# A one-core decoder layer: norm factors in PSUM, x in halves, four projection tiles moved, sums of weights one at a time

## The chip, the cores and the metric

The kernel runs on one core of a Trainium2 chip, all arithmetic in fp32. The metric is the device time of one launch in microseconds. TensorE is PE here, VectorE DVE, ScalarE ACT, GpSimd POOL, and SP is the engine that issues the DMAs.

## What is computed

One step of a decoder layer for a prompt of 1024 tokens and 8 samples of 4 tokens, 1056 columns in all, model width 1024:

```
hn  = rms_norm(x, norm_mix_pre)
mix = hybrid_mixer(hn, states)            # three head groups, one output projection w_out
x   = x + rms_norm(mix, norm_mix_post)
hn  = rms_norm(x, norm_ffn_pre)
gate, val = split(hn @ w_up)              # 1024 -> 2 x 2816
gate = causal_dwconv(gate)                # width 3
f   = (gelu(gate) * val) @ w_down         # 2816 -> 1024
y   = x + rms_norm(f, norm_ffn_post)
```

and the updated states of prompt and samples.

## The kernel before

Activations lie transposed: 128 of the 1024 features on the partitions, tokens along the free axis. The 1056 columns are cut into four quarters of 264 (Q). A weight tile is 128 outputs wide; it is loaded in fp32, cast by ACT to a rounded high part wh, and the remainder wl is a subtraction on POOL or DVE (`load_w`, L263 to L273). A product (`dense`, L275) takes three matmuls for each of 8 k-steps: high by high, high by low, low by high, 24 matmuls for one tile and one quarter.

PE's order is the order in which the program emits its instructions. The other engines are ordered by a scheduler from emission order and priorities; `tc.high_priority(offset=n)` moves instructions n places ahead. The emission is done by `Weave` (L121): each stream is a generator with a rank, it yields the nanoseconds or the condition that it waits for, and a virtual clock (`weave.now`) is advanced by the matmuls emitted. The stream of lowest rank that is due goes next, so streams of high rank fill the gaps. The due times are the table WAIT.

The stages that matter:

- **Samples.** The samples' states are worked through in `sample_gdn`, `sample_ssd` and `sample_ml` (ranks 3 to 5), while `project_first` (L1638, rank 9) fills the gaps with w_out's products for quarters 0 and 1. Behind the first tile it splits quarter 2's input (`split_mix(2)`: two casts, two subtractions).
- **Projection.** `project_last` (L1656) does all eight tiles for quarters 2 and 3. Its weights, and the first four gate tiles of w_up (`load_up`), are loaded between the products. `product` (L1592) has ACT read a result from PSUM twice (L1596, L1599), and POOL sums the squares of two tiles at a time (L1601). PSUM has two banks in `accp`, one in `sump`, and in this stage five in `accr`.
- **Norms.** `finish(q)` (L1603, rank 8) waits for the quarter before, loads x of the quarter into the one tile x, and makes the factor r of the first norm with `rstd_of` (L310): two matmuls with ones, logarithm and exponential on ACT, r in SBUF. Then mix is scaled (L1616), x added (L1617), squared and summed (L1620, L1624), x1 written to DRAM, and after `f_rows[q]` nanoseconds the second norm follows: its sum on PE, r, a product (L1634) and a split in two parts (L1580, L1581).
- **Up projection.** Four gate tiles are done as plain products, quarter by quarter (`up`, L1930), into the four fpre tiles of `new_pre` (L1802; POOL sets their first columns at L1779). `pieces` (L1703) makes seven combinations of the input's halves, and the other tiles are done in pairs by a scheme of seven products (class `fast`, L1867): a task is a pair of gate or of value tiles, its steps (p, u) are product p for half u of the columns, 12 matmuls each. Products 4 and 3 of a task are done within the steps of the next task. `weights(p)` makes the weight combinations on DVE (L1883, L1884, L1886, L1888), priority AHEAD = 400, then casts and subtracts (L1849, L1850). Results leave PSUM through DVE (L1824, L1826, L1833 for value tiles).
- **Down projection.** w_down is done in six parts; L2016 adds a product onto fa. In the last part `final(q)` (L2026) scales fa by the norm's weights on ACT (L2030), makes r, and multiplies and adds x on DVE and POOL (L2034, L2035).

Of the kernel before, what the change touches and what calls it, by code (L numbers as in the profile page):

```python
# [73 lines left out]
    s_norm=6310, rows1=9000, rows2=6960, rows3=8500, f_rows=(24000, 15500, 15500, 12500), f_wait=7000, f_piece=2600,  # L74
# [123 lines left out]
def kernel(ctx: ExitStack, tc: tile.TileContext, I, O):  # L198
# [111 lines left out]
    def rstd_of(r, ssum):  # L310

        ps = sump.tile([P, 512], F32, name="po")
        n = r.shape[-1]
        for s in ssum:
            mm(ps[:, :n], lhsT=ones, rhs=s, start=(s is ssum[0]), stop=(s is ssum[-1]))
        log = nc.scalar.activation(out=r, in_=ps[:, :n], func=AF.Ln, scale=1.0 / D, bias=epsc)
        in_order(log, tables[-1])
        nc.scalar.activation(out=r, in_=r, func=AF.Exp, scale=-0.5)
        return r
# [51 lines left out]
    with ExitStack() as ph:  # L371
# [1220 lines left out]
        def product(m, w, q):  # L1592
            if m == 0:
                sqs[q] = on.tile([P, 2, Q], F32, name="ss", bufs=4)
            ps = yield from dense(accp if q < 2 else accr, w, operand, KS, q, Q)
# [7 lines left out]
        def finish(q):  # L1603
            if q:
                yield lambda: ("x", q - 1) in have
            x = on.tile([P, KD, Q], F32, name="x")
            dma(out=x, in_=I["xQ"][q])
            yield WAIT["f_wait"]
            s = sqs[q]
            r = rstd_of(on.tile([P, Q], F32, name="rstd", bufs=2), [s[:, 0, :], s[:, 1, :]])  # L1610
            sx = on.tile([P, KH, Q], F32, name="sx")
            s = on.tile([P, 2, Q], F32, name="ss", bufs=4)
            for i in range(2):
# [3 lines left out]
                vtt(out=x[:, ks], in0=x[:, ks], in1=m, op=ALU.add)  # L1617
                if i == 0:
                    act(out=sx, in_=x[:, ks], func=AF.Square)
                    vtt(out=sx[:, 0:2], in0=sx[:, 0:2], in1=sx[:, 2:4], op=ALU.add)  # L1620
                else:
                    for a in (KH, KH + 2):
                        act(out=sx[:, 2:4], in_=x[:, a:a + 2], func=AF.Square)
                        vtt(out=sx[:, 0:2] if a == KH else s, in0=sx[:, 0:2], in1=sx[:, 2:4], op=ALU.add)  # L1624
                dma(out=x1_dram[q, :, ks], in_=x[:, ks])
            for k in range(KD):
                act(out=mix[k][:, quarters[q]], in_=x[:, k, :], func=AF.Copy, scale=col(V_FPRE + k))
            have.add(("x", q))
            yield WAIT["f_rows"][q]
            r = rstd_of(on.tile([P, Q], F32, name="rstd", bufs=2), [s[:, 0, :], s[:, 1, :]])  # L1630
# [7 lines left out]
        def project_first():  # L1638
            for m in range(KD):
                w = load_w(I["w_out"][m], KD)  # L1640
                for q in range(2):
                    yield from product(m, w, q)
                if m == 0:
                    split_mix(2)
# [529 lines left out]
```

## Time and profile before

| | us |
|---|---|
| median of 3 runs | 1590.47 |
| lowest, highest | 1586.07, 1594.12 |
| the profiled execution | 1597.13 |
| its span | 1595.3 |
| PE busy | 1480.2 (93%) |
| DVE busy | 1014.4 (64%) |
| ACT busy | 621.1 (39%) |
| POOL busy | 581.2 (36%) |

Times in the rows are microseconds from the span's start. A row of the timeline has the start, the duration, the engine, the line, the operation with its output and inputs, the count where rows are merged, and in brackets the idle time before it with the instruction that ended it. Matmul ends are modelled, so that consecutive matmuls overlap in their rows.

### The profile page before, as it was taken

What the parts mean: (1) busy time and instruction counts of PE and PEld (TensorE: products, weight loads), DVE (VectorE), ACT (ScalarE), POOL (GpSimd) and SP (SyncE); (2) the same over time, 40 slices, a digit from 0 to 9 for tenths busy, and PEclk for the clock granted to TensorE, in tenths of its full rate; (3) what the DMA queues carried; (4) which work ended last, traced back from release to release, by engine and by line L of the source; (5) the groups of instructions that cost most, each with busy time, mean ns of one, the idle gap of its engine ahead of it and who ended that gap; (6) DMA issues with size and microseconds to landing.
All of it is one profiled execution on the core that took longest, in us unless ns stands there. A gap on an engine that the chain in (4) does not pass through costs nothing. (4 is left out here: it accounts for less than half of the span.)

```text
span 1595.3 us, 27520 instructions
## 1 busy us (share of the span) xinstructions
PE 1480.2 (93%) x10756; PEld 1430.2 (90%) x10756; DVE 1014.4 (64%) x2019; ACT 621.1 (39%) x1348; POOL 581.2 (36%) x666
## 2 busy tenths in 40 slices
PE   9888998989989989998599999999999999999995
PEld 8888898979989889887499999999999999999995
DVE  6898878795484367513688766666666675234457
ACT  7643544433432332413556533333333344112244
POOL 6344333232444542437240533333332332212323
PEclk9899999999999999769799999999999999999998
DMA  6110111011121232213531212221222226312303
GB/s 217 33 45 29 32 37 37 22 30 30 56 61 40 69 112 83 68 53 98 196 110 57 77 59 67 81 81 68 81 74 75 81 92 233 122 50 94 119 28 137
DMA packets 59786, 124.92 MB, mean 78 GB/s; under 512 B 15480, under 2 KB 21496, under 8 KB 58632
## 3 DMA queue, kind: packets, MB, share of 16 engines
q1 hardware_dynamic: 59656, 123.16, 23.2%
q8 instruction: 85, 1.39, 0.4%
q14 instruction: 45, 0.37, 0.1%
HBM read 97.40 MB, written 25.21 MB: 77 GB/s over the span
## 5 line engine op out<-in xcount | busy, mean ns | idle before, releaser
L208 PE MATMUL acc<-h,wh 128*128 128x264 f32 (+1 forms) x3040 | 687.1, 317 | 15.8 <-DVE pre L308 11.7
L208 PEld LDWEIGHTS acc<-h,wh 128*128 128x128 f32 x3040 | 505.4, 195 | 23.3 <-DVE pre L308 8.0
L208 PE MATMUL acc<-h,wl 128*128 128x264 f32 (+1 forms) x1528 | 471.4, 308 | 2.9 <-POOL wl L272 2.4
L208 PEld LDWEIGHTS acc<-h,wl 128*128 128x128 f32 x1528 | 295.5, 193 | 3.9 <-POOL wl L272 2.6
L208 PE MATMUL acc<-hidl,wh 128*128 128x264 f32 x576 | 163.7, 284 | 0.5 <-DVE hidl L1993 0.5
L208 PE MATMUL acc<-hidh,wh 128*128 128x264 f32 x576 | 163.9, 285 | 0.0
L208 PE MATMUL acc<-hidh,wl 128*128 128x264 f32 x576 | 163.5, 284 | 0.0
L1850 POOL TENSOR_TENSOR wl<-ws,wh 128x512 fp32r<-128x512 f32 x60 | 77.6, 1301 | 191.2 <-ACT wh L1849 191.2
L2016 DVE TENSOR_TENSOR fa<-fa,acc 128x264 f32<-128x264 f32 x160 | 68.0, 427 | 124.5 <-PE acc L208 123.7
L272 POOL TENSOR_TENSOR wl<-w,wh 128x1024 fp32r<-128x1024 f32 x42 | 104.7, 2493 | 54.3 <-ACT wh L271 50.8
L208 PE MATMUL acc<-n,wh 128*128 128x264 f32 x640 | 119.3, 283 | 0.0
L208 PEld LDWEIGHTS acc<-hidl,wh 128*128 128x128 f32 x576 | 108.5, 188 | 0.8 <-DVE hidl L1993 0.8
L208 PEld LDWEIGHTS acc<-hidh,wl 128*128 128x128 f32 x576 | 108.6, 189 | 0.0
L208 PEld LDWEIGHTS acc<-hidh,wh 128*128 128x128 f32 x576 | 108.5, 188 | 0.0
L208 PE MATMUL acc<-r,wh 128*128 128x264 f32 x480 | 91.0, 287 | 13.3 <-DVE rs L1826 13.3
L2007 POOL TENSOR_TENSOR wl<-w,wh 128x1024 fp32r<-128x1024 f32 (+1 forms) x22 | 47.6, 2163 | 148.3 <-ACT wh L2006 145.4
L208 PEld LDWEIGHTS acc<-n,wh 128*128 128x128 f32 x640 | 98.8, 188 | 0.2 <-issue 0.2
L208 PE MATMUL acc<-n,wl 128*128 128x264 f32 x320 | 92.0, 288 | 3.1 <-POOL wl L1850 3.1
L1850 POOL TENSOR_TENSOR wl<-w,wh 128x512 fp32r<-128x512 f32 x40 | 59.2, 1488 | 81.8 <-ACT wh L1849 81.8
L208 PEld LDWEIGHTS acc<-r,wh 128*128 128x128 f32 x480 | 74.3, 188 | 15.4 <-DVE rs L1826 15.2
L1786 DVE SCALAR_TENSOR_TENSOR fy<-fpre,vec,fy 128x1072 f32<-128x1072 f32 x44 | 67.3, 1548 | 14.9 <-ACT fy L217 14.8
L2006 ACT CAST wh<-w 128x1024 fp32r<-128x1024 f32 (+1 forms) x22 | 20.5, 933 | 131.7 <-PE acc L208 127.0
(527 smaller groups left out, 3073.2 us busy)
## 6 DMA issues: line engine op xcount, KB each, us to landing
w<-in_w_in_dram SPq DMA_DIRECT2D x30, 512.0 KB
w<-in_w_up_dram SPq DMA_DIRECT2D x60, 256.0 KB
hid_dram<-hid SPq DMA_DIRECT2D x22, 528.0 KB
hidl<-hid_dram SPq DMA_DIRECT2D x21, 528.0 KB
w<-in_w_dn_dram SPq DMA_DIRECT2D x17, 512.0 KB
w<-in_w_out_dram SPq DMA_DIRECT2D x16, 512.0 KB
E<-rows_dram SPq DMA_DIRECT2D x24, 256.0 KB
n<-in_w_up_dram SPq DMA_DIRECT2D x20, 256.0 KB
```

Source lines behind the costliest of these rows:

```text
L208: return nc.tensor.matmul(out, **kw)
L272: tt(out=wl[:, ks], in0=w[:, ks], in1=wh[:, ks].bitcast(F32), op=ALU.subtract)
L1786: stt(out=y[:, :LF], in0=pre[:, j:j + LF], scalar=col(V_FW + 3 * f + j), in1=y[:, :LF], op0=ALU.mult, op1=ALU.add)
L1850: tt(out=wl, in0=x, in1=wh.bitcast(F32), op=ALU.subtract)
L2006: nc.scalar.copy(out=wh, in_=w)
L2007: gtt(out=wl, in0=w, in1=wh.bitcast(F32), op=ALU.subtract)
L2016: vtt(out=fa[:, q, m, :], in0=fa[:, q, m, :], in1=ps[:, :Q], op=ALU.add)
```

## The change

- `rstd_of` can leave r in the PSUM bank of its sum. All factors of `finish` and `final` do so, the first of `finish` in `sump`, the others in `accp`.
- x of a quarter is loaded in two halves, x0 and x1. Quarter 1 has homes of its own in two fpre tiles, from when the left pool is closed. The due times f_rows change.
- `project_first` also does tiles 0 to 3 for quarter 2; weights 2 and 3 are held in the homes h4 to h7 of quarter 1's operands. `split_mix(2)` is behind the fourth tile, and the second tile's load is raised by 300 places. `project_last` loads tiles 4 to 7 at its start and does those for quarter 2, then all eight for quarter 3. Tiles 4 and 7 take their subtraction on DVE.
- The four sums of weights of a task are methods of their own, called one by one between steps at normal priority; the next task's tiles are allocated and loaded from the fifth step of the one before, and its outputs' tiles at first use.
- `final` multiplies by the norm's weights and r in one DVE instruction; the adds are on POOL, except six of the last quarter's on DVE.

```diff
@@ -71,7 +71,7 @@
     ssd_unit=6650, ssd_post=2800, s_decay=3970, state=430, s_hop=2530, outer=760, s_ml=3230, s_out=2100,
-    s_norm=6310, rows1=9000, rows2=6960, rows3=8500, f_rows=(24000, 15500, 15500, 12500), f_wait=7000, f_piece=2600,
+    s_norm=6310, rows1=9000, rows2=6960, rows3=8500, f_rows=(20000, 22000, 16000, 12500), f_wait=7000, f_piece=2600,
 )
@@ -307,13 +307,15 @@
-    def rstd_of(r, ssum):
-        ps = sump.tile([P, 512], F32, name="po")
-        n = r.shape[-1]
+    def rstd_of(r, ssum, pool=sump, name="po"):
+        n = ssum[0].shape[-1]
+        ps = pool.tile([P, 512], F32, name=name)[:, :n]
         for s in ssum:
-            mm(ps[:, :n], lhsT=ones, rhs=s, start=(s is ssum[0]), stop=(s is ssum[-1]))
-        log = nc.scalar.activation(out=r, in_=ps[:, :n], func=AF.Ln, scale=1.0 / D, bias=epsc)
+            mm(ps, lhsT=ones, rhs=s, start=(s is ssum[0]), stop=(s is ssum[-1]))
+        r = ps if r is None else r
+        log = nc.scalar.activation(out=r, in_=ps, func=AF.Ln, scale=1.0 / D, bias=epsc)
         in_order(log, tables[-1])
@@ -1589,10 +1591,10 @@
-        def product(m, w, q):
+        def product(m, w, q, pool):
             if m == 0:
                 sqs[q] = on.tile([P, 2, Q], F32, name="ss", bufs=4)
-            ps = yield from dense(accp if q < 2 else accr, w, operand, KS, q, Q)
+            ps = yield from dense(pool, w, operand, KS, q, Q)
             act(out=mix[m][:, quarters[q]], in_=ps[:, :Q], func=AF.Copy, scale=col(V_NPOST + m))
@@ -1601,33 +1603,37 @@
         def finish(q):
-            if q:
-                yield lambda: ("x", q - 1) in have
-            x = on.tile([P, KD, Q], F32, name="x")
-            dma(out=x, in_=I["xQ"][q])
+            yield lambda: "left" in have if q == 1 else q == 0 or ("x", q - 1) in have
+            xs = [new_pre()[:, :KH * Q].rearrange("p (k g) -> p k g", k=KH) if q == 1 else
+                  on.tile([P, KH, Q], F32, name=f"x{i}") for i in range(2)]
+            for i in range(2):
+                dma(out=xs[i], in_=I["xQ"][q][:, KH * i:KH * i + KH])
+            if q == 1:
+                yield lambda: ("x", 0) in have
             yield WAIT["f_wait"]
             s = sqs[q]
-            r = rstd_of(on.tile([P, Q], F32, name="rstd", bufs=2), [s[:, 0, :], s[:, 1, :]])
+            r = rstd_of(None, [s[:, 0, :], s[:, 1, :]])
             sx = on.tile([P, KH, Q], F32, name="sx")
...
                 vtt(out=m, in0=m, in1=bc(r, 1, KH), op=ALU.mult)
-                vtt(out=x[:, ks], in0=x[:, ks], in1=m, op=ALU.add)
+                vtt(out=xs[i], in0=xs[i], in1=m, op=ALU.add)
+                dma(out=x1_dram[q, :, ks], in_=xs[i])
                 if i == 0:
-                    act(out=sx, in_=x[:, ks], func=AF.Square)
+                    act(out=sx, in_=xs[i], func=AF.Square)
                     vtt(out=sx[:, 0:2], in0=sx[:, 0:2], in1=sx[:, 2:4], op=ALU.add)
                 else:
-                    for a in (KH, KH + 2):
-                        act(out=sx[:, 2:4], in_=x[:, a:a + 2], func=AF.Square)
-                        vtt(out=sx[:, 0:2] if a == KH else s, in0=sx[:, 0:2], in1=sx[:, 2:4], op=ALU.add)
-                dma(out=x1_dram[q, :, ks], in_=x[:, ks])
+                    for a in (0, 2):
+                        act(out=sx[:, 2:4], in_=xs[i][:, a:a + 2], func=AF.Square)
+                        vtt(out=s if a else sx[:, 0:2], in0=sx[:, 0:2], in1=sx[:, 2:4], op=ALU.add)
             for k in range(KD):
-                act(out=mix[k][:, quarters[q]], in_=x[:, k, :], func=AF.Copy, scale=col(V_FPRE + k))
+                act(out=mix[k][:, quarters[q]], in_=xs[k // KH][:, k % KH], func=AF.Copy, scale=col(V_FPRE + k))
             have.add(("x", q))
             yield WAIT["f_rows"][q]
-            r = rstd_of(on.tile([P, Q], F32, name="rstd", bufs=2), [s[:, 0, :], s[:, 1, :]])
+            r = rstd_of(None, [s[:, 0, :], s[:, 1, :]], accp, "acc")
             new_operand(q)
@@ -1635,43 +1641,52 @@
+        def tile_w(t):
+            return t[:, :D].rearrange("p (k c) -> p k c", c=P)
+        held = {}
+        def hold(m, parts=None):
+            held[m] = load_w(I["w_out"][m], KD, parts=parts, tt=vtt if m in (4, 7) else gtt)
...
             for m in range(KD):
-                w = load_w(I["w_out"][m], KD)
+                with tc.high_priority(offset=300) if m == 1 else nullcontext():
+                    w = load_w(I["w_out"][m], KD)
                 for q in range(2):
-                    yield from product(m, w, q)
-                if m == 0:
+                    yield from product(m, w, q, accp)
+                if m == 3:
                     split_mix(2)
...
             for m in range(2):
-                held[m] = load_w(I["w_out"][m], KD)
+                hold(m)
+            for m in range(2, 4):
+                hold(m, [tile_w(hnp.tile([P, T], F32R, name=f"h{2 * m + i}")) for i in range(2)])
+            for m in range(4):
+                yield from product(m, held[m], 2, accp)
             have.add("half")
...
-        def tile_w(t):
-            return t[:, :D].rearrange("p (k c) -> p k c", c=P)
-        held = {}
...
             def load(m):
-                parts = [tile_w(new_n((2 * m + 4) % 12 + i)) for i in range(2)]
-                held[m] = load_w(I["w_out"][m], KD, parts=parts, tt=vtt if m % 2 else gtt)
+                hold(m, [tile_w(new_n(2 * m - 8 + i)) for i in range(2)])
...
                 held["up", f] = load_w(I["w_up"][2 * f], KD, parts=parts)
-            load(2)
+            for m in range(4, KD):
+                load(m)
             split_mix(3)
-            for q in (2, 3):
-                for m in range(KD):
-                    yield from product(m, held[m], q)
-                    if q == 2 and m + 3 < KD:
-                        load(m + 3)
-                    if q == 3 and m < PLAIN:
-                        load_up(m)
-                weave.add(finish(q), 8)
+            for m in range(4, KD):
+                yield from product(m, held[m], 2, accr)
+            weave.add(finish(2), 8)
+            for m in range(KD):
+                yield from product(m, held[m], 3, accr)
+                if m < PLAIN:
+                    load_up(m)
+            weave.add(finish(3), 8)
             have.add("projected")
@@ -1697,6 +1712,8 @@
+        have.add("left")
@@ -1709,6 +1726,8 @@
                 X[u][p] = hi, lo
+            for q in range(2 * u, 2 * u + 2):
+                yield lambda: ("normed", q) in have
             vtt(out=B[0][0], in0=B[0][1], in1=B[0][0], op=ALU.subtract)
@@ -1732,7 +1751,8 @@
             yield from pieces(0, {p: [(fn, f"n{2 * i + j}") for j in range(2)] for i, p in enumerate((6, 5, 7, 4))})
-            yield lambda: ("normed", 3) in have
+            for q in range(NQ):
+                yield lambda: ("normed", q) in have
             onstack.close()
@@ -1803,9 +1823,11 @@
         def gate_task(i):
-            pres = [new_pre() for j in range(2)]
+            pres = []
...
             def out(j, h, u, x, ps):
+                if not pres:
+                    pres.extend(new_pre() for j in range(2))
                 gate_in(pres[j], 2 * u + h, x, ps)
@@ -1814,9 +1836,11 @@
         def value_task(i):
-            hids = [fo[0].tile([P, T], F32, name="hid", bufs=2) for j in range(2)]
+            hids = []
...
             def out(j, h, u, x, ps):
+                if not hids:
+                    hids.extend(fo[0].tile([P, T], F32, name="hid", bufs=2) for j in range(2))
                 q = 2 * u + h
@@ -1872,20 +1896,26 @@
                 self.A = [[w[j][:, KH * r:KH * r + KH] for j in range(2)] for r in range(2)]
-                for r, j in ((0, 0), (1, 0), (1, 1), (0, 1)):
+                for r, j in ((1, 0), (1, 1), (0, 0), (0, 1)):
                     dma(out=self.A[r][j], in_=I["w_up"][2 * (2 * i + r) + val][:, KH * j:KH * j + KH])
...
+            def sum_of(self, n):
+                A = self.A
+                if n == 0:
+                    self.s = [fo[0].tile([P, KH, P], F32, name="ws", bufs=3)]
+                    vtt(out=self.s[0], in0=A[1][0], in1=A[1][1], op=ALU.add)
+                elif n == 1:
+                    self.s.append(fo[0].tile([P, KH, P], F32, name="ws", bufs=3))
+                    vtt(out=self.s[1], in0=self.s[0], in1=A[0][0], op=ALU.subtract)
+                elif n == 2:
+                    vtt(out=A[1][0], in0=A[0][0], in1=A[1][0], op=ALU.subtract)
+                else:
+                    vtt(out=self.s[1], in0=A[0][1], in1=self.s[1], op=ALU.subtract)
...
                 A = self.A
-                if p == 6:
-                    self.s = [fo[0].tile([P, KH, P], F32, name="ws", bufs=3) for j in range(2)]
-                    vtt(out=self.s[0], in0=A[1][0], in1=A[1][1], op=ALU.add)
-                    vtt(out=self.s[1], in0=self.s[0], in1=A[0][0], op=ALU.subtract)
-                elif p == 7:
-                    vtt(out=A[1][0], in0=A[0][0], in1=A[1][0], op=ALU.subtract)
-                elif p == 3:
-                    vtt(out=self.s[1], in0=A[0][1], in1=self.s[1], op=ALU.subtract)
                 x = {1: A[0][0], 2: A[0][1], 4: A[1][1], 7: A[1][0]}.get(p)
@@ -1946,15 +1976,18 @@
             prev = None
+            following = tasks[0][0](tasks[0][1])
+            for k in range(2):
+                following.sum_of(k)
             for n, (task, i) in enumerate(tasks):
-                cur = task(i)
+                cur = following
                 if n == 0:
...
                             drain(gate_conv(2 * i + j, pres[2 * i + j], ys[i][j]))
-                for p, u in ((1, 0), (1, 1), (6, 0), (4, 0), (4, 1), (3, 0), (6, 1), (3, 1),
-                             (5, 0), (5, 1), (2, 0), (2, 1), (7, 0), (7, 1)):
+                for at, (p, u) in enumerate(((1, 0), (1, 1), (6, 0), (4, 0), (4, 1), (3, 0), (6, 1), (3, 1),
+                                             (5, 0), (5, 1), (2, 0), (2, 1), (7, 0), (7, 1))):
                     if p in (4, 3):
@@ -1964,6 +1997,13 @@
                         one_later()
+                    if at in (0, 8):
+                        cur.sum_of(3 if at else 2)
+                    elif n + 1 < len(tasks):
+                        if at == 4:
+                            following = tasks[n + 1][0](tasks[n + 1][1])
+                        elif at in (9, 10):
+                            following.sum_of(at - 9)
                 prev = cur
@@ -2026,13 +2066,12 @@
             dma(out=x, in_=x1_dram[q])
+            r = rstd_of(None, ssum[q], accp, "acc")
             for k in range(KD):
-                act(out=fa[:, q, k, :], in_=fa[:, q, k, :], func=AF.Copy, scale=col(V_FPOST + k))
-            r = rstd_of(fp.tile([P, Q], F32, name="rstd", bufs=2), ssum[q])
-            for k in (0, 2, 1, 3, 4, 6, 5, 7):
-                tt = gtt if k in ((2, 5) if q == NQ - 1 else (1, 2, 5)) else vtt
-                tt(out=fa[:, q, k, :], in0=fa[:, q, k, :], in1=r, op=ALU.mult)
-                tt(out=x[:, k, :], in0=x[:, k, :], in1=fa[:, q, k, :], op=ALU.add)
+                y = fa[:, q, k, :]
+                stt(out=y, in0=y, scalar=col(V_FPOST + k), in1=r, op0=ALU.mult, op1=ALU.mult)
+                tt = vtt if q == NQ - 1 and k not in (1, 4) else gtt
+                tt(out=x[:, k, :], in0=x[:, k, :], in1=y, op=ALU.add)
                 yield
...
```

## Rows read from the trace of the kernel before

**Rows 1.** The page, its slices of the span

```profile
PEclk9899999999999999769799999999999999999998
```

**Rows 2.** What PE waited for: us, times, longest

```profile
PE po L208 <- DVE ss L1624: 15.4, 1, 15.4
PE acc L208 <- DVE rs L1826: 13.3, 9, 1.7
...
PE acc L208 <- POOL wl L1850: 3.6, 11, 0.6
```

**Rows 3.** Windows by stage: length, busy PE PEld DVE ACT POOL, clock, DMA

```profile
640.00:658.00 18.00, 14.52 (x105) 13.65 (x103) 16.54 (x34) 14.02 (x30) 6.95 (x6) 1.00 0.26 85
658.00:704.00 46.00, 46.00 (x211) 41.58 (x212) 4.96 (x16) 6.72 (x17) 17.93 (x19) 0.50 0.13 45
704.00:749.00 45.00, 43.74 (x324) 39.51 (x323) 14.25 (x26) 13.69 (x36) 30.05 (x20) 0.98 0.25 83
749.00:762.00 13.00, 9.17 (x23) 3.84 (x23) 7.22 (x10) 4.75 (x7) 6.55 (x4) 0.87 0.48 162
762.00:782.00 20.00, 18.57 (x148) 18.02 (x146) 18.50 (x13) 13.04 (x22) 8.59 (x4) 1.00 0.59 194
782.00:804.00 22.00, 6.24 (x18) 4.87 (x19) 8.67 (x9) 11.63 (x27) 2.59 (x2) 0.55 0.53 190
804.00:888.00 84.00, 81.55 (x654) 80.64 (x654) 69.77 (x53) 52.13 (x96) 28.75 (x26) 1.00 0.21 73
```

**Rows 4.** Windows, two tasks of the up projection

```profile
993.40:1036.62 43.22, 41.26 (x338) 40.84 (x337) 28.06 (x50) 14.62 (x24) 14.79 (x19) 1.00 0.22 75
```

**Rows 5.** Timeline, the wait in that period

```profile
992.24 1.76 DVE L1883 TENSOR_TENSOR ws<-w 128x512 f32<-128x512 f32 x1 [1.43 <-POOL wl L1850]
...
995.47 0.42 DVE L1826 TENSOR_TENSOR rs<-n,acc 128x264 f32<-128x264 f32 x1
...
995.94 0.51 PE L208 MATMUL acc<-r,wh 128*128 128x264 f32 x2 [1.65 <-DVE rs L1826]
```

**Rows 6.** Timeline, w_out's second tile

```profile
653.47 3.21 POOL L272 TENSOR_TENSOR wl<-w,wh 128x1024 fp32r<-128x1024 f32 x1 [0.71 <-POOL kqM L1389]
...
656.73 0.39 PE L208 MATMUL acc<-h,wl 128*128 128x264 f32 x1 [2.37 <-POOL wl L272]
```

**Rows 7.** Timeline of PE, state matmuls of the samples

```profile
662.02 0.85 PE L208 MATMUL mc<-kqS,kq 128*128 128x8 f32 x4
...
664.20 0.85 PE L208 MATMUL mc<-kqS,kq 128*128 128x8 f32 x4
...
708.72 0.51 PE L208 MATMUL mc<-kqG,h 128*128 128x8 f32 x4
...
709.89 0.51 PE L208 MATMUL mc<-kqG,h 128*128 128x8 f32 x4
```

**Rows 8.** Timeline, the second quarter's x and sum

```profile
764.63 0.10 POOL L1779 MEMSET fpre<- 128x2 f32 x1 [7.92 <-DMA out_gdn_s_dram<-kq]
...
791.19 2.43 DVE L1617 TENSOR_TENSOR x<-x,mix 128x1056 f32<-128x1056 f32 x2 [8.72 <-DMA x<-in_xQ_dram]
...
797.19 2.13 PE L208 MATMUL po<-ss,ones 128*128 128x264 f32 x4 [15.40 <-DVE ss L1624]
```

**Rows 9.** Two source lines: count, ns minimum/median/maximum, forms

```profile
L2034 DVE TENSOR_TENSOR fa<-fa,rstd x21: 417/426/984, 1544.9 to 1591.3; 128x264 f32<-128x264 f32 x21
...
L2016 DVE TENSOR_TENSOR fa<-fa,acc x160: 412/429/431, 1332.3 to 1582.7; 128x264 f32<-128x264 f32 x160
```

**Rows 10.** Timeline, the end of the span

```profile
1577.12 0.42 DVE L2016 TENSOR_TENSOR fa<-fa,acc 128x264 f32<-128x264 f32 x1
...
1582.88 1.25 PE L208 MATMUL po<-fs,ones 128*128 128x264 f32 x2 [5.85 <-DVE fs L350]
...
1586.07 1.32 DVE L2034 TENSOR_TENSOR fa<-fa,rstd 128x264 f32<-128x264 f32 x2 [2.56 <-ACT rstd L318]
...
1591.69 0.76 DVE L2035 TENSOR_TENSOR xf<-xf,fa 128x264 f32<-128x264 f32 x2
```

## The prediction

> **What bounds the kernel now.** I read the page's slices first: TensorE (PE) is busy nine tenths of the span, and its granted clock falls in slices 17 to 20, some 640 to 800 us [rows 1]. So PE is the bound almost everywhere, and only two things can shorten the run: PE waiting, and PE at its lower clock. The list of what PE waited for gives the places [rows 2]: 15.4 us once, for the sums of the second norm (L1624), 13.3 us in nine waits on L1826, 3.6 us in eleven on weight pieces. [...] The nine waits lie in the up projection, one per two tasks [rows 4, 5]. The end has its own loss: PE's last product is read at 1577.12 and the span ends at 1595.3 [rows 10].
>
> The sum is made against the profiled execution's own 1597.1 us (span 1595.3 and 1.8 around it). That is 6.7 above the median shown and 3 above the highest of the three.
>
> **Sums of weights one by one.** Now DVE runs L1883, L1884 and L1886 as a block. In the even task it starts at 992.24, the first takes 1.76 us, and L1826, which empties a PSUM bank, comes behind it at 995.47; PE takes that bank at 995.94 after 1.65 us idle [rows 5]. After the change the same four sums per task are issued one at a time: two after the products (5,1) and (2,0) of the task before, two after (1,0) and (5,0) of their own. None is left in the two steps between (4,0), whose result frees the bank, and (6,1), which takes it. A period is 43.22 us, PE is busy 41.26 of it, DVE 28.06 [rows 4], so DVE has room for 0.7 us more in other steps. Nothing is added. Also moved are the two tiles' four DMAs per task: they are emitted ten steps earlier on SP, but a tile must be free first, so they start when they start now. I take 13 us off. Ends: 17 off (all waits on sums and pieces), 5 added (new waits of 0.25 us in each of 20 tasks).
>
> **The second output weight first.** PE waits 2.37 us at 656.73 for the low part of w_out's second tile, which POOL starts only at 653.47 and needs 3.21 us for [rows 6]. Raised in priority, and with the third quarter's split (two ACT casts, two DVE subtractions) moved behind the fourth tile, its cast goes ahead of the splits. POOL had idled 0.71 us ahead of it [rows 6], so the cast is what it waits for. 2.4 us off; ends 0 and 3.5 (all idle time of 640 to 658 [rows 3]).
>
> **The clock.** The granted clock falls at the end of that same idle spell and stays at half to 704 [rows 3]. From one group of state matmuls to the next, with two steps of a product between them, are 2.18 us there, and 1.17 us in the same mixture at full clock behind it [rows 7]. At 709 the mixture does not bring the clock down; the idle spell ahead of it is what differs. Without the spell, 46 us become 46 x 1.17 / 2.18 = 24.7, 21 less. At full clock the chains of the samples have less time: from 704 to 749 PE idled 1.3 us [rows 3]; I leave 3 for that and take 18 off. Ends: 0 (it falls anyway) and 21.
>
> **Four products among the samples, and the norms.** From 749 to 804 lie 55 us. PE is busy 9.17 + 18.57 + 6.24 = 34 of them [rows 3], some 8 of that at half clock, so the work is 30 us at full clock and 25 us are lost: to the last sample steps with nothing between them, to the 15.4 us wait [rows 8], and to the half clock behind it. The wait comes from x: the second quarter's load has one home with the first's, DVE gets it only at 791.19 after 8.72 us, and in PE's order its second sum stands ahead of work that is ready [rows 8]. The change attacks all of it. Four products of the third quarter, 24 matmuls at 41.26/338 = 0.122 us [rows 4] = 2.9 us each, 11.7 in all, fill the samples' end; as much leaves the stage behind. Each brings what it brought there (one 512 KB DMA, a cast, a subtraction, two ACT reads, half a POOL sum); tiles 2 and 3 take the homes of the second quarter's operands, free after the sixteenth product. The second quarter's x gets its own home, and the due times put its sum behind the first's (20.0 against 7 + 22.0 after a later start, not 24.0 against 22.5).
>
> Not all 25 us come back. The x halves land in fpre tiles, whose first write now waits for the samples' state going out, until 764.6 [rows 8]; on SP, loads of w_out tiles 4 to 7 may queue behind the two DMAs, and PE would wait for tile 4: some 5 us. Tile 7 stays on DVE and tile 4 comes to it, tiles 3 and 5 go to POOL. And DVE is busy 104.2 us in 749 to 888 (four rows of the table added [rows 3]): with 25 us less it would be busy 104 of 114. I take 20 off. Ends: 0 and 27 (with the 2.5 us idle in 804 to 888).
>
> **Factors in PSUM.** Now r lies in SBUF: the same 264-element product takes DVE 417 to 984 ns with it (L2034), but 412 to 431 with an operand in PSUM (L2016) [rows 9], in the same stretch where POOL multiplies and adds. So r in PSUM costs nothing by rows and frees these operations from the long form; I count 0, ends 0 and 3 us less. [...]
>
> **The last norm.** Per quarter eight ACT copies go, the scale joins the product on DVE (8 instead of 5 or 6), and the adds go to POOL except six of the last quarter. DVE falls behind now: PE waits 5.85 us for its sum at 1582.88, runs it at half clock, and r is read at 1586.07 [rows 10]. After: bank read 0.42 at 1577.1, square 0.42, sum 0.55, logarithm 0.48, exponential 0.42, hand-overs 0.3: r near 1579.7. Then 14 DVE operations at 0.34 to 0.98 instead of 12: 6.3 us, as now (1586.07 to 1592.45). 6 us off; ends 2 and 9. The other quarters' are hidden under PE.
>
> Edits with one answer: x in two DMAs instead of one adds an issue on SP, x1's halves leave before the squares, pieces wait also for earlier quarters, tiles of a task are allocated at first use. None is on PE's path.
>
> Sum: 1597.1 - 13 - 2.4 - 18 - 20 - 6 = 1537.7, say **1538**.
>
> **Rivals.** (1) The clock falls all the same, at the transposes before the state steps or at a wait that full speed brings: 18 us back, 1556. For it: the stretch 749 to 762, idle for 4 of 13 us, has a clock of 0.87 [rows 3], so shorter idle spells bring it down too. Against it: the one long idle spell ahead of this stretch goes. (2) The finish is bound by DVE or by x instead of PE, and the 20 us come back as waits at po: 1558. For it: DVE at 104 of 114 us. Against: 16 factor products leave the contended form. (1) and (2) together: 1576. (3) The sums' move does nothing, because PE then waits for the weight pieces' two tile pairs in the same step: 1551. For it: 3.6 us of such waits exist. (4) Slower: the sums lose their priority; a first sum issued after (5,1) has seven steps of 1.46 us = 10.2 us to become a piece (sum 0.7, cast 0.6, subtraction 1.3), 7.6 to spare. If DVE runs later than that, every us is paid in each of 20 tasks; beyond 59/20 = 3 us, a backlog of 10.6, the run is slower than before, at 4 us 1618. DVE's 28 us in 43 speak against it.
>
> **How the numbers follow.** Forecast (1526 to 1548) 0.42, (1) 0.22, (2) 0.15, both 0.08, (3) 0.05, (4) 0.05, more than forecast 0.03. The range 1520 to 1570 leaves out the cases both, (4) and some of the last, 0.16. A measurement here can tell 0.5%, 8 us: only (4) and the edge of both end above 1582, so 0.90 faster, 0.05 the same, 0.05 slower.
>
> **What would show it.** Periods of 41.6 us in the up projection with no wait on L1826; no wait on the second w_out tile and a granted clock of 1.00 from 640 on; no wait of over 5 us on L1624; the up projection starting 40 us earlier; r of the last quarter read within 3 us of PE's last product. A row of half clock of over 20 us in the samples, or po waiting for L1624, proves the step wrong; periods of 43 us prove the largest sure term wrong.

## The result, and the profile after

The kernel after takes 1548.74 us (median of 4 runs, 1547.99 to 1549.13), the kernel before beside it 1588.27 (1582.6 to 1594.12): a ratio of 0.975, interval 0.9712 to 0.9788. The profiled executions stand at 1549.13 and 1597.13, 48.0 apart; the forecast had 59.4 off that execution, and 1538. The profiled execution of the kernel before is one of its slow ones, with a mean granted clock of 0.959 where its executions of 1569 to 1576 us show 0.974 to 0.979 and the kernel after 0.977 to 0.979, so that about half of the 48.0 is a loss that the kernel before does not always have.

To see where the 48.0 lie, I cut PE's timeline at five rows that all kernels here have: the first and the last group of state matmuls of the samples (mc<-kqS,kq and mc<-kqG,kq), the first product of the up projection's pairs with an operand r, the first of the down projection (hidl), the last matmul of the last product. A stretch runs from the start of one row to the start of the next. The same cuts serve for all runs below, since the spread of the kernel before (1569 to 1600 us over all its runs) is larger than most effects. The expectations count B from the last matmul of the group that opens it, which gives 152.5 for after where the table, from the first, has 152.8.

| stretch, us | before | after | less | forecast |
|---|---|---|---|---|
| up to the first state matmuls | 657.7 | 657.3 | 0.4 | 2.4 |
| A: state matmuls | 71.1 | 50.2 | 20.9 | 18 |
| B: samples' end, projection, norms, plain tiles | 160.5 | 152.8 | 7.7 | 20 |
| C: pairs of the up projection | 440.4 | 427.7 | 12.7 | 13 |
| D: down projection | 247.2 | 246.7 | 0.4 | 0 |
| E: from the last matmul of the last product to the end | 18.6 | 12.6 | 6.0 | 6 |

The page's slices of after, beside [rows 1]:

```profile
PEclk9989999999999999999899999999999999999998
```

The one slice of 8 among the norms takes the place of a 7, a 6, a 9 and a 7. The table by stage, beside [rows 3] and with its columns:

```profile
640.00:658.00 18.00, 14.78 (x105) 13.71 (x104) 16.10 (x33) 13.75 (x29) 6.70 (x6) 1.00 0.32 104
658.00:704.00 46.00, 46.00 (x363) 41.22 (x362) 11.07 (x27) 13.12 (x36) 31.01 (x28) 1.00 0.20 70
704.00:749.00 45.00, 40.74 (x282) 35.86 (x282) 19.24 (x28) 18.23 (x39) 28.37 (x18) 1.00 0.40 133
749.00:762.00 13.00, 6.52 (x34) 6.22 (x35) 10.74 (x6) 7.18 (x14) 7.55 (x4) 0.61 0.81 271
762.00:782.00 20.00, 20.00 (x157) 19.61 (x156) 11.98 (x10) 12.99 (x28) 6.01 (x3) 1.00 0.44 166
782.00:804.00 22.00, 20.95 (x167) 20.48 (x166) 17.56 (x13) 16.25 (x34) 11.84 (x5) 1.00 0.49 171
804.00:888.00 84.00, 77.25 (x605) 75.91 (x604) 71.27 (x77) 46.51 (x79) 22.95 (x28) 0.96 0.16 52
```

From 658 to 704 PE does 363 matmuls where it did 211, at 1.00 instead of 0.50. But 640 to 658 has about as much idle time as it had (14.78 busy against 14.52), and new losses stand at 749 to 762 and behind 804. PE's waits name them (us in all, times, longest):

```profile
PE acc L208 <- DVE ss L1631: 5.7, 2, 4.6
...
PE acc L208 <- ACT n L271: 5.2, 1, 5.2
...
PE acc L208 <- DVE n L272: 3.7, 1, 3.7
...
PE acc L208 <- DVE rs L1850: 2.8, 8, 0.4
PE acc L208 <- POOL wl L1874: 2.7, 9, 0.3
...
PE acc L208 <- DVE h L1583: 2.4, 1, 2.4
```

Against [rows 2]: the 15.4 us for the second quarter's second sum are gone; 8.9 us for the weight of tile 4 (n) and 4.6 for the last quarter's second sum are new; the nine waits on a bank (L1826 before, L1850 now) fell from 13.3 to 2.8. The second w_out tile costs no wait, but 2.4 us for a split (h L1583) stand in its place.

The loop. Two tasks of the up projection, a window of the kind in [rows 4], and DVE's timeline ahead of the wait that [rows 5] show:

```profile
963.97:1005.85 41.88, 41.23 (x337) 40.81 (x337) 29.38 (x50) 14.72 (x24) 17.16 (x18) 1.00 0.23 77
```

```profile
1000.43 1.78 DVE L1915 TENSOR_TENSOR ws<-n,ws 128x512 f32<-128x512 f32 x1
1002.14 1.77 DVE L1908 TENSOR_TENSOR ws<-w 128x512 f32<-128x512 f32 x1
1003.83 0.42 DVE L1948 TENSOR_TENSOR n<-n,acc 128x264 f32<-128x264 f32 x1
1004.17 0.68 DVE L1911 TENSOR_TENSOR ws<-ws,w 128x512 f32<-128x512 f32 x1
1004.78 0.68 DVE L1913 TENSOR_TENSOR w<-w 128x512 f32<-128x512 f32 x1
1005.38 0.41 DVE L1850 TENSOR_TENSOR rs<-n,acc 128x264 f32<-128x264 f32 x1
```

The period fell from 43.22 to 41.88. DVE does not spread the sums in this task: four sums still run just ahead of L1850, and the same block stands in every second task. But it no longer begins with 1.43 us idle, and PE's wait behind it is 0.34 (1005.85) instead of 1.65.

The end, DVE's timeline, beside [rows 10]:

```profile
1536.33 0.42 DVE L2056 TENSOR_TENSOR fa<-fa,acc 128x264 f32<-128x264 f32 x1
...
1538.96 0.89 DVE L2072 SCALAR_TENSOR_TENSOR fa<-fa,vec,acc 128x264 f32<-128x264 f32 x2 [1.81 <-ACT acc L320]
...
1544.00 0.43 DVE L2074 TENSOR_TENSOR xf<-xf,fa 128x264 f32<-128x264 f32 x1
```

PE's last matmul begins at 1534.70 and ends at 1534.98; its bank is read at 1536.33, r at 1538.96, 4.3 us behind that start. In the kernel before it was 9.3 (1576.75 to 1586.07). There the row at 1577.12 in [rows 10] reads an earlier product's bank. The last one was read only here, 5.7 us behind the last matmul's end, where after takes 1.35:

```profile
1582.74 0.42 DVE L2016 TENSOR_TENSOR fa<-fa,acc 128x264 f32<-128x264 f32 x1
```

### The profile page after: what moved, and what is told of

The parts are those of the page before. It is cut to its first block, busy times and chain, and to the rows that moved or that the text cites. A ratio compares the mean times of both kernels' runs of the same rounds, so it can differ in the third digit from the quotient of the medians.

```text
span 1547.3 us, 27515 instructions
## 1 busy us (share of the span) xinstructions
PE 1456.2 (94%) x10756; PEld 1410.7 (91%) x10756; DVE 1019.2 (66%) x2014; ACT 605.3 (39%) x1316; POOL 604.0 (39%) x671
## 5 line engine op out<-in xcount | busy, mean ns | idle before, releaser
L208 PE MATMUL acc<-h,wh 128*128 128x264 f32 (+1 forms) x3040 | 677.2, 313 | 17.5 <-DVE pre L308 12.3
L208 PEld LDWEIGHTS acc<-h,wh 128*128 128x128 f32 x3040 | 496.6, 191 | 24.4 <-DVE pre L308 8.7
L208 PE MATMUL acc<-h,wl 128*128 128x264 f32 (+1 forms) x1528 | 466.2, 305 | 0.3 <-POOL wl L619 0.2
L208 PEld LDWEIGHTS acc<-h,wl 128*128 128x128 f32 x1528 | 290.5, 190 | 1.5 <-POOL wl L619 1.5
L1874 POOL TENSOR_TENSOR wl<-ws,wh 128x512 fp32r<-128x512 f32 x60 | 89.3, 1495 | 161.0 <-ACT wh L1873 156.4
L1874 POOL TENSOR_TENSOR wl<-w,wh 128x512 fp32r<-128x512 f32 x40 | 64.9, 1625 | 81.0 <-ACT wh L1873 75.3
L1806 DVE SCALAR_TENSOR_TENSOR fy<-fpre,vec,fy 128x1072 f32<-128x1072 f32 x44 | 75.1, 1730 | 3.2 <-ACT fy L217 2.7
```

Source lines behind the costliest of these rows:

```text
L208: return nc.tensor.matmul(out, **kw)
L1806: stt(out=y[:, :LF], in0=pre[:, j:j + LF], scalar=col(V_FW + 3 * f + j), in1=y[:, :LF], op0=ALU.mult, op1=ALU.add)
L1874: tt(out=wl, in0=x, in1=wh.bitcast(F32), op=ALU.subtract)
```

## The experiments

All twelve in stretches A to E, from one profile each; medians are in the text.

| run | A | B | C | D | E |
|---|---|---|---|---|---|
| before, again | 68.8 | 160.4 | 438.9 | 247.0 | 18.6 |
| before, sums alone changed | 59.3 | 160.9 | 428.8 | 247.5 | 18.6 |
| after, no priority | 50.2 | 154.0 | 427.1 | 247.0 | 12.6 |
| after, split back | 50.2 | 152.9 | 427.1 | 246.7 | 12.6 |
| after, both back and old final | 50.2 | 153.7 | 427.6 | 247.1 | 18.7 |
| after, r in SBUF | 50.2 | 157.9 | 427.2 | 246.9 | 16.9 |
| after, none early | 50.2 | 144.0 | 428.8 | 246.1 | 12.6 |
| after, one home | 50.2 | 144.3 | 427.9 | 247.0 | 12.6 |
| after, neither | 50.2 | 144.9 | 428.9 | 246.7 | 12.6 |
| after, first sum at once | 50.9 | 145.9 | 428.3 | 246.7 | 12.6 |
| after, six early | 50.2 | 152.8 | 427.2 | 247.0 | 12.6 |
| after, third quarter's sum later | 50.2 | 154.7 | 427.5 | 246.9 | 12.6 |

**The kernel before, again.** No edit.

> The kernel before once more, for a second profile. If the fall of the granted clock at 658 us belongs to the kernel (an idle spell of 2.4 us ahead of it), this profile shows 0.50 from 658 to 704 again and a time of 1582 to 1598 us. If it came by chance in the one execution that was profiled, the stretch is at 1.00 and the span some 20 us shorter.

1596.16 us, a clock of 0.50 from 659 to 703: the fall came in both profiles of this kernel, so it is not the chance of one execution. By the mean clocks given above it is shorter or absent in the executions of 1569 to 1576 us, of which there is no profile.

**The sums alone.** The loop's part of the diff on the kernel before: `sum_of`, the place of its calls, the earlier tiles and the order of their four loads, the output tiles at first use.

```diff
+            following = tasks[0][0](tasks[0][1])
...
-                cur = task(i)
+                cur = following
...
+                    if at in (0, 8):
+                        cur.sum_of(3 if at else 2)
+                    elif n + 1 < len(tasks):
+                        if at == 4:
+                            following = tasks[n + 1][0](tasks[n + 1][1])
+                        elif at in (9, 10):
+                            following.sum_of(at - 9)
```

> The kernel before with the sums of weights alone changed (one by one, tiles ten steps earlier, output tiles at first use). Theory: the nine waits on L1826 came from the block of three sums, so they go without the other edits: 13 us less than before, a period of 41.9 us. Rival (3): pieces' waits take their place, under 3 us less. Rival: the waits went only because the rest of DVE's work moved, no change.

Median 1573.82, ratio 0.9905 (0.9851 to 0.9959). C is 11.6 us shorter than in the first profile of before and 10.1 than in the second, against 12.7 and 11.2 in after: the loop's gain is the sums' own. Which of its parts takes the wait, the place of the sums or the earlier tiles, was not tried apart. The rest of the span's difference is the clock, which fell here too, but for 20 us only:

```profile
656.00:658.00 2.00, 2.00 (x12) 2.00 (x12) 2.00 (x6) 0.00 (x0) 2.00 (x3) 0.58 0.64 207
658.00:676.00 18.00, 18.00 (x82) 17.57 (x82) 1.42 (x4) 2.64 (x6) 8.32 (x9) 0.50 0.10 36
676.00:678.00 2.00, 2.00 (x16) 1.61 (x15) 0.29 (x1) 0.27 (x1) 1.70 (x1) 0.80 0.00 0
678.00:704.00 26.00, 26.00 (x194) 21.74 (x195) 6.38 (x17) 6.75 (x19) 11.86 (x13) 1.00 0.22 82
```

PE is at 100% all through, and nothing in these rows marks the return at 676. That the fall is shorter here is not shown to be the edit's doing: the ten executions of this run range from 1559.79 to 1587.38 us, at mean clocks of 0.977 to 0.958.

**No priority.**

```diff
-                with tc.high_priority(offset=300) if m == 1 else nullcontext():
-                    w = load_w(I["w_out"][m], KD)
+                w = load_w(I["w_out"][m], KD)
```

> The kernel after without the raised priority of w_out's second tile; the third quarter's split stays behind the fourth tile. If the order of POOL's and DVE's queues by priority is what keeps the clock up, PE waits over 2 us for the second tile at some 655 and the clock falls to 0.50 for some 40 us: 18 to 21 us slower than after. If the place of the split alone does it, the time of after within 2 us.

**Split back.**

```diff
-                if m == 3:
+                if m == 0:
                     split_mix(2)
```

> The kernel after with the third quarter's split back behind the first tile; the raised priority stays. If the two casts and two subtractions of the split are what delays PE at 650 to 657, the clock falls again: 18 to 21 us slower than after. If the priority alone does it, the time of after within 2 us.

Medians 1543.14 and 1546.93: no slower than after, and A is 50.2 in both. With either edit undone by itself, the clock stays up. Without the priority PE is even earlier: from its last 352-column product to the first state matmul are 9.8 us, against 12.8 in after and 12.8 to 14.7 in all other runs. DVE's timelines tell why, first after, then the run without priority:

```profile
647.62 2.42 DVE L429 SCALAR_TENSOR_TENSOR mix<-pre 128x32 f32<-128x32 f32 x1
...
651.02 1.25 DVE L1583 TENSOR_TENSOR h<-mix,h 128x1056 fp32r<-128x1056 f32 x1
```

```profile
644.55 0.49 DVE L429 SCALAR_TENSOR_TENSOR mix<-pre 128x32 f32<-128x32 f32 x1
...
645.36 1.24 DVE L1583 TENSOR_TENSOR h<-mix,h 128x1056 fp32r<-128x1056 f32 x1
```

Raised, the weight's subtraction runs on POOL from 646.61 to 649.99, and an instruction of 32 columns on DVE takes 2.42 us beside it instead of 0.49. The split behind it is late, and PE waits 2.42 us for that. The edit moved the wait from one product to another. Without it the same subtraction runs at 647.89, and an instruction of 128 columns on DVE takes 2.27 us beside it, but PE waits 0.43 at most. With both edits undone, in the next run, the stretch is 13.8: the later split alone gains some 4 us, and the priority gives 3 of them back.

**Both back, and the old final().** The two diffs above, and `final` as in the kernel before.

```diff
-                stt(out=y, in0=y, scalar=col(V_FPOST + k), in1=r, op0=ALU.mult, op1=ALU.mult)
-                tt = vtt if q == NQ - 1 and k not in (1, 4) else gtt
...
+                tt = gtt if k in ((2, 5) if q == NQ - 1 else (1, 2, 5)) else vtt
+                tt(out=fa[:, q, k, :], in0=fa[:, q, k, :], in1=r, op=ALU.mult)
```

> The kernel after with three edits back that lie in two stretches far apart, read stretch by stretch: neither the raised priority nor the later split (together now), and final() as it was. From the first state matmul to the last of its mixture: if either of the two edits alone keeps the clock up, as their single runs say, the fall comes back with both gone, and this stretch is 60 to 71 us instead of 50.2; if something else keeps it up, it stays at 50.2. From PE's last product to the end: 18.5 us instead of 12.6 if final() alone made the gain there; r stands in SBUF in this part.

Median 1555.04. E is 18.7: `final`, with the place of its r, makes the whole gain at the end. A is 50.2 once more, so in this profile the two edits undone do not bring the long fall back. But the run does not restore the spell of [rows 6]: PE waits 1.19 us for the second tile's low part where the kernel before has 2.37. PE's timeline, first after, then this run:

```profile
652.32 0.39 PE L208 MATMUL acc<-h,wh 128*128 128x264 f32 x1 [2.42 <-DVE h L1583]
```

```profile
654.43 0.39 PE L208 MATMUL acc<-h,wl 128*128 128x264 f32 x1 [1.19 <-POOL wl L272]
```

In the three profiles with the long fall a wait of 2.35 to 2.37 us ends 1.0 to 1.7 us ahead of the first state matmul; in the eleven others no wait of over 1.2 us ends in the last 4.9 us ahead of it (in after it is 652.32 against 657.31). So the spell right ahead of the state matmuls stays a candidate, which no run put back in full. And one of this run's four executions took 1570.2 us at a mean clock of 0.964, the others 1554.5 to 1555.3 at 0.976 to 0.978; it was not profiled, so whether the long fall came back in it is not known. In the profile the clock does fall, but early:

```profile
650.00:651.00 1.00, 0.61 (x3) 0.61 (x4) 1.00 (x6) 1.00 (x3) 0.00 (x0) 0.75 0.00 0
651.00:653.00 2.00, 2.00 (x11) 1.93 (x9) 2.00 (x3) 1.02 (x7) 1.83 (x1) 0.50 0.00 0
653.00:654.00 1.00, 0.24 (x2) 0.00 (x0) 1.00 (x1) 1.00 (x3) 1.00 (x1) 0.54 0.00 0
654.00:655.00 1.00, 0.57 (x4) 0.57 (x5) 1.00 (x4) 0.53 (x1) 0.84 (x2) 1.00 0.00 0
```

It is back before the state matmuls begin at 655.39.

**r in SBUF.** All factors in tiles named rstd, on the same PSUM pools.

```diff
-            r = rstd_of(None, [s[:, 0, :], s[:, 1, :]])
+            r = rstd_of(on.tile([P, Q], F32, name="rstd", bufs=2), [s[:, 0, :], s[:, 1, :]])
...
-            r = rstd_of(None, ssum[q], accp, "acc")
+            r = rstd_of(fp.tile([P, Q], F32, name="rstd", bufs=2), ssum[q], accp, "acc")
```

> The kernel after with every factor of the norms in SBUF instead of PSUM, nothing else moved. Forecast's term: 0, with 0 to 3 us slower by the long form of DVE's products beside POOL. [...] From the state steps to the first task of the up projection, 152.5 us, no change within 2 us.

Median 1558.58; B 5.1 and E 4.4 us longer than in after, and r's place is the only edit. The forecast's 0 to 3 fell. Two source lines of this run, then the same of after (count, ns minimum/median/maximum):

```profile
L1622 DVE TENSOR_TENSOR mix<-mix,rstd x8: 1246/1254/3428, 740.9 to 822.6; 128x1056 f32<-128x1056 f32 x8
...
L2072 DVE SCALAR_TENSOR_TENSOR fa<-fa,vec,rstd x32: 479/488/970, 1506.2 to 1550.7; 128x264 f32<-128x264 f32 x32
```

```profile
L1622 DVE TENSOR_TENSOR mix<-mix,po x8: 1240/1245/1254, 742.9 to 819.8; 128x1056 f32<-128x1056 f32 x8
...
L2072 DVE SCALAR_TENSOR_TENSOR fa<-fa,vec,acc x32: 472/480/490, 1503.3 to 1543.5; 128x264 f32<-128x264 f32 x32
```

With r in PSUM not one of these products is long (1254 and 490 ns at most); with r in SBUF some take two or three times as long (up to 3428 and 970). In B two products (3428 and 2376 ns) add 3.3 us; the rest of the 5.1 is not accounted for one by one, since some splits and additions with both operands in SBUF are long in either run (up to 3.46 us here, 3.48 in after, where others of the same size take 1.25). At the end the last bank is read 4.1 us behind the last matmul's end instead of 1.35, and PE waits 4.20 us at 1542.02 for the last quarter's sum, which DVE adds up behind these products.

**None early.**

```diff
-            for m in range(4):
-                yield from product(m, held[m], 2, accp)
             have.add("half")
...
-            for m in range(4, KD):
+            for m in range(KD):
                 yield from product(m, held[m], 2, accr)
```

> The kernel after with the four products of the third quarter back behind the samples; their weights stay in their new homes. Theory: the four are 11.7 us of cover, so PE stands idle 11.7 us longer ahead of the fourth tile's weight less what is hidden there, and falls to the lower clock behind it: 8 to 14 us slower than after. Rival: the wait for the fifth tile's weight (8.9 us) swallows them, since the four products then run while that weight is made: within 3 us of after.

**One home.**

```diff
-            yield lambda: "left" in have if q == 1 else q == 0 or ("x", q - 1) in have
-            xs = [new_pre()[:, :KH * Q].rearrange("p (k g) -> p k g", k=KH) if q == 1 else
-                  on.tile([P, KH, Q], F32, name=f"x{i}") for i in range(2)]
+            if q:
+                yield lambda: ("x", q - 1) in have
+            xs = [on.tile([P, KH, Q], F32, name=f"x{i}") for i in range(2)]
...
-            if q == 1:
-                yield lambda: ("x", 0) in have
```

> The kernel after with the second quarter's x back in the one pair of homes, loaded when the first quarter's x is used up. Theory: the own home is what took the wait of 15.4 us on the second sum, so this wait comes back in good part: 8 to 15 us slower than after. Rival: the due times and the four products took it, and the load now lands in time: within 3 us of after.

Medians 1540.43 and 1540.64, ratios 0.9756 and 0.9765: their B is 8.8 and 8.5 us shorter than in after, where every theory said longer or the same. The norms' sums on PE's timeline show what changed. After, then one home:

```profile
765.91 1.05 PE L208 MATMUL po<-ss,ones 128*128 128x264 f32 x4
...
791.11 1.05 PE L208 MATMUL acc<-ss,ones 128*128 128x264 f32 x4
...
807.12 1.16 PE L208 MATMUL po<-ss,ones 128*128 128x264 f32 x4 [1.49 <-POOL fpre L1799]
826.71 1.69 PE L208 MATMUL acc<-ss,ones 128*128 128x264 f32 x3 [4.62 <-DVE ss L1631]
```

```profile
755.68 1.96 PE L208 MATMUL po<-ss,ones 128*128 128x264 f32 x4
...
783.56 1.05 PE L208 MATMUL acc<-ss,ones 128*128 128x264 f32 x4
...
804.22 1.05 PE L208 MATMUL po<-ss,ones 128*128 128x264 f32 x4
819.74 1.16 PE L208 MATMUL acc<-ss,ones 128*128 128x264 f32 x4 [0.68 <-DVE ss L1629]
```

These are the second quarter's two sums and the fourth quarter's two. In after the second quarter's first sum is 10 us later (9.4 counted from the end of A): its 7 us of due time (`f_wait`) run only from the closing of the left pool, and in PE's order it stands behind some 65 matmuls of tiles 4 to 6 that follow it otherwise. Its second norm then falls together with the third quarter's and the pieces; DVE is busy without a gap from 801 to 826, and PE waits for the fourth quarter's sum.

**First sum at once.**

```diff
-            yield WAIT["f_wait"]
+            yield 0 if q == 1 else WAIT["f_wait"]
```

> The kernel after with the second quarter's first sum due at once instead of 7 us after its condition; the only change is its place in PE's order, 66 matmuls earlier, and that of its second sum, 66 earlier too. Theory: the condition on the left pool made this due time start late, all four norms follow each other on DVE, and so the fourth quarter's second sum comes 8 us late; its 4.6 us wait and the lower clock behind it go, 8 to 10 us off the stretch from the state steps to the first task (152.5 us), and with x in a home of its own at least as good as with the one home (144.3 us). Rival: x of the second quarter comes too late for the earlier sum to help, under 3 us.

Median 1545.23, B 145.9: 6.9 us less, by the place of one sum in PE's order. The wait at the fourth quarter's sum is 1.25. With the sum in nearly the same place (252 matmuls behind the state matmuls, 255 with one home), the own home gives nothing over the one home.

**Neither.** Both undone.

> The kernel after with neither the four early products nor the second quarter's own home for x; each undone alone took 8.5 us off the stretch from the state steps to the first task (152.5 to 144.0 and 144.3). Theory: the two cost 8.5 together only because the early products move the left pool's end, and with it the second quarter's first sum, 66 matmuls back; neither gains by itself, so with both undone the stretch is 142 to 147 us, and what the stretch gained since before comes from the factors in PSUM, the order of the due times and the halves. Rival: one covers for the other, and with both undone the 15 us wait for x comes back: over 152 us.

Median 1541.36, B 144.9, as the theory said. The 15 us wait does not come back; PE's longest in this stretch is 4.9 us, for a state of the samples (h L1352).

**Six early.** Tiles 4 and 5 in h8 to h11, the fourth quarter's operand in n0 to n3 (`new_operand`), and the loops of `project_last` from 6.

```diff
-            for m in range(2, 4):
+            for m in range(2, 6):
                 hold(m, [tile_w(hnp.tile([P, T], F32R, name=f"h{2 * m + i}")) for i in range(2)])
-            for m in range(4):
+            for m in range(6):
                 yield from product(m, held[m], 2, accp)
```

> The kernel after with six products of the third quarter among the samples instead of four: tiles 4 and 5 in the homes h8 to h11, the fourth quarter's operand in n0 to n3. Theory: PE's 8.9 us idle at 746 to 756 wait for weights whose home is free only when the last state has gone out, so two products more (5.8 us) fill it, and the stretch at the lower clock behind it shrinks: 6 to 10 us faster than after. Rival: PE then waits just as long for the fourth quarter's split or the next tile: within 2 us of after.

Median 1550.03, B 152.8: the rival. The wait for tile 4's weight (n) went and two others came, 5.0 us for ACT to read a bank (sq L217) and 4.3 for another (ss L217), since ACT's queue stood at squares that waited for DVE (4.75 us until 749.01, 3.90 until 784.65); the wait for the fourth quarter's second sum is 5.2.

**Third quarter's sum later.**

```diff
-f_rows=(20000, 22000, 16000, 12500)
+f_rows=(20000, 22000, 22000, 12500)
```

> The kernel after with the third quarter's second sum due 22 us after its first instead of 16. Theory: the 4.6 us wait at 822 to 827, with the lower clock behind it, is a due time set too early while other products are ready: 4 to 7 us faster than after. Rival: DVE is the bound from 804 to 827, the wait moves to the next thing that it makes: within 2 us of after.

Median 1549.5, B 154.7. A miss of mine: the wait at 822 to 827 is the fourth quarter's, whose due time is the last entry, and PE's wait there grew to 7.0.

## Why the prediction was right, and where not

The range held, the sign and most of the size. That the total comes within 11 us of 1538 is in part luck: the norms missed by 12 us although 5.1 us of the factors, a term put at nothing, lie in them, and the sum starts 6.7 us above the median. Step by step:

- **Sums of weights one by one:** 13 forecast, 12.7 measured, and 10 to 12 shown for the edit alone. "None is left in the two steps" failed: DVE keeps the block, and by the rows it is the earlier start that takes the wait (1.43 us idle ahead of the block gone, 1.31 us less wait behind it); no run shows that part alone. The forecast's period of 41.6 is 41.88.
- **The second output weight first:** 2.4 forecast, 0.4 measured, and that is no gain: two profiles of the kernel before have 657.7 and 660.7 in this row, and from the last 352-column product on both kernels take 12.8. The step "its cast goes ahead of the splits" was right and its price was missed: beside POOL's subtraction an instruction of DVE for the samples takes 2.42 us, 0.49 in the run without the priority, and PE waits 2.42 us for a split behind it.
- **The clock:** 18 forecast, 20.9 between these two profiles. The size held between these two; the cause I gave is not shown. The idle time of 640 to 658 did not go (14.78 us busy of 18 against 14.52), in after it lies earlier, and neither edit that I held responsible brings the long fall back in a profile, singly or together, though no run put the whole spell back. Three profiles with the samples as before show a fall at 656 to 659, as the state matmuls begin, of 48, 44 and 20 us. In the eleven of the changed kernel and its variants it does not come (three) or comes at 648 to 655 and is over within 7 us (eight), in all but one ahead of the state matmuls. Which of the edits does that stays open. The term is worth 20.9 only against the execution that was profiled.
- **Four products among the samples, and the norms:** 20 forecast, 7.7 measured; here the forecast missed its 12 us. The failing step is "Four products of the third quarter ... fill the samples' end" together with "The second quarter's x gets its own home". The samples' end is filled, but tile 4's weight then keeps PE waiting 8.9 us where I had put 5 into the term, and, not foreseen, the condition on the left pool puts the second quarter's sum some 65 matmuls back. With both undone B is 7.9 us shorter. That the wait of 15.4 us went is then the work of other edits: the factors in PSUM give 5.1, and what is left, some 10 us if the parts add up, lies with the due times, the halves and the order of the loads, which I did not try apart.
- **Factors in PSUM:** 0 forecast (bounds 0 and 3 us less), 9.5 measured, 5.1 in B and 4.4 in E. The reading of [rows 9] held: with r's place the only edit, the longest products take 3.43 us with r in SBUF and 1.25 in PSUM (L1622), 0.97 and 0.49 (L2072). I priced it by the 21 instructions of the kernel before; in the changed one POOL does 26 of the 32 last adds beside DVE's products, and with r in SBUF the long forms stand on the path. The common form costs nearly the same: L2072 has a median of 480 ns with r in PSUM and 488 in SBUF.
- **The last norm:** 6 forecast, 6.0 measured, r read 2.6 us behind the last bank as worked out, though that bank itself is read 1.35 us behind the product's end. The prediction misread the row at 1577.12 as the last bank's; that was read at 1582.74, so the larger part of the gain, 4.4 us, is that DVE comes to the last bank earlier. And 4.4 of the 6.0 need r in PSUM: with r in SBUF the new `final` saves 1.7 only.

Rival (1) did not come, in the sense that the clock stayed up in A; rival (2) came in part, as DVE's queue behind a late sum. Rivals (3) and (4) fell with C. Of the signs, no wait on L1631, which stands for L1624, is over 5 us (4.6). But the clock was 0.61 at 749 to 762, the up projection starts 29 us earlier instead of 40, and r is read 4.0 us behind PE's last matmul, not within 3.

The median fell by 39.5 and the profiled execution by 48.0, mainly because A of the kernel before varies: it was 71, 69 and, in the run with the sums, 59. Where the kernel before shows the mean clock of after (0.977 to 0.979, five executions of 1569 to 1575 us), the difference is 20 to 27 us.

Three variants beat both kernels: none early, one home and neither, each with a B of some 144 us, 8 less than after, at medians of 1540 to 1541. They were not timed beside after, whose four executions lie at 1548 to 1549. Leaving out the raised priority as well (3 us ahead of the state matmuls by its run) was not tried with them.

## What to carry to other kernels

A due time that is counted from a condition moves when the condition does: when work is put ahead of the end of a stage, see which sums then stand behind it in PE's order, and by how many matmuls (some 65 here). Filling one idle spell pays only if the next thing that is late is known; here two edits that each fill a gap cost 8 us together. Where an operand of DVE stands is worth trying by itself: at the end here, where POOL's adds run beside DVE's products, r in PSUM was worth more than the structure around it (4.4 us against 1.7). And a raised priority has a price to look for: beside the subtraction that it moved ahead on POOL, a short instruction of DVE took 2.42 us instead of 0.49.

## What the runs showed that I had not expected

A DVE instruction of 128x32 took 2.42 us beside a POOL subtraction of 3.38 us, and 0.49 without that. A product of 128x1056 with its factor in SBUF took up to 3.43 us, and 1.25 at most with the factor in PSUM. The low clock of the state stretch lasted 48, 44 and 20 us in three profiles with a PE busy all the time; no row shows what ended it.
